# Splitting the attention projections' weights on GpSimd instead of VectorE

## The chip, the core and the metric

The program runs on one core of a Trainium2 chip. The metric is the device time of one execution, in microseconds (us). The engines are called PE (TensorE: matmuls, with PEld for its weight loads), DVE (VectorE), ACT (ScalarE), POOL (GpSimd) and SP (SyncE, which here issues most of the DMAs).

## What is computed

Two decoder layers for a prompt of 1024 tokens and for 8 sample tokens that share the weights. Each layer takes an RMS norm of x, projects it with one weight matrix, runs four heads of differential attention beside four heads of gated linear attention, projects the result back, and adds a SwiGLU block. The part that matters here is the projection of the four attention heads:

```python
n = rmsnorm(yp, norm1[l])          # (y * g): g is norm1, one value per input feature
z = n @ w_in_l                     # 1024 features in, D_IN columns out
dq, dk, dv, gq, gk, gv, gg, gr = jnp.split(z, cuts, axis=-1)
q = rope(rmsnorm(dq.reshape(B, T, DIFF_HEADS, 2, DIFF_DK), q_norm_l), pos)
k = rope(rmsnorm(dk.reshape(B, T, DIFF_HEADS, 2, DIFF_DK), k_norm_l), pos)
v = dv.reshape(B, T, DIFF_HEADS, DIFF_DV)
```

Each head needs 128 columns each of q, k and v. The kernel multiplies in a shortened float format (fp32r), so it splits both operands of each product in a high and a low part and adds three products: high by high, low by high, high by low.

## The kernel before

Each layer runs three stages one after the other. Stage D (`phase_d`, line 384) does the attention heads, stage G (`phase_g`) the gated linear attention, and stage F the output projection and the SwiGLU block, with the attention of the sample tokens over the paged cache laid beside it. In layer 0 stage D takes the time from the start to about 285 us, in layer 1 from about 1400 to 1666 us.

In stage D the heads come one after the other (line 586). For each head, `head(h)` (line 403) prepares the weights of the head, and returns three functions: `proj(i)` projects tile i of 128 tokens (i = 8 is the tile of the 8 sample tokens), `attend(i)` does the scores, the softmax and the product with v of tile i, and `finish` normalises the head's output. The loop issues `proj(0)`, `proj(1)`, the sample tile, and `proj(2)` to `proj(7)`; two attention tiles stay pending (`LAG`, line 45), so the attention of tile i follows `proj(i + 2)`, and the last tiles of a head fall beside the first projections of the next. `head(h + 1)` is called behind `proj(3)` of head h.

The weights of a head are prepared by `prep_cols` (line 212) in eight steps, k = 0 to 7, one for each 128 input features. A step loads `raw`, 128 rows by 384 columns (400 for head 3, which also carries the 16 columns of the gate's low rank part, loaded by a second DMA), from SP's queue. ACT writes `wh = raw * g` rounded to fp32r, where g is one value for each partition out of `g1c`. DVE writes `wl = raw * g - wh` with one scalar_tensor_tensor (the helper `stt`, line 137, whose instructions the profile shows at line 138). There are 4 buffers of `raw`, and 9 each of `wh` and `wl`. So one step of the next head can be prepared ahead, and the other seven wait until the last projection of the head before, `proj(7)`, has read its eight steps one after the other; and the `raw` of a step is loaded when the split four steps earlier has been done.

`proj(i)` is `gemm_tok` (line 236): for each step k three matmuls into one accumulator of PSUM (`psq`; there are 3 of these), xH by wh, xL by wh, and xH by wl. What follows each projection on ACT and DVE are the squares, the norm and the rotation of q and k, the copy of v, and DMAs of k and v to the outputs; then PE transposes q and k.

The tile framework orders each engine's instructions when the program is built: it plans by priority (the order of the program text) among the instructions that its plan has as ready, and on the chip each engine then works through its list in that order. The order on PE, ACT, DVE, POOL and SP is thus fixed before the run, and it can come out otherwise when an instruction moves to another engine.

The helper `tt` (line 134) is a tensor_tensor, on DVE unless another engine is given; the profile shows its instructions at line 135. `bc` (line 140) broadcasts an operand.

Of the kernel before, what the change touches and what calls it, by code (L numbers as in the profile page):

```python
# [16 lines left out]
ALU = mybir.AluOpType  # L17
# [4 lines left out]
P = 128  # L22
# [20 lines left out]
RANK = 16  # L43
# [9 lines left out]
C_Q, C_K, C_V = 0, 512, 1024  # L53
# [4 lines left out]
def f(ap):  # L58
    return ap.bitcast(F32)
# [3 lines left out]
def hybrid_kernel(  # L63
# [8 lines left out]
    PE, ACT, DVE, POOL, SP = nc.tensor, nc.scalar, nc.vector, nc.gpsimd, nc.sync  # L72
# [14 lines left out]
    def act(out, in_, func, **kw):  # L87
        return ACT.activation(out, in_, func, **kw)  # L88
# [45 lines left out]
    def tt(out, a, b, op, eng=None):  # L134
        return (eng or DVE).tensor_tensor(out, a, b, op=op)  # L135

    def stt(out, in0, scalar, in1, op0, op1, eng=None):
        (eng or DVE).scalar_tensor_tensor(out=out, in0=in0, scalar=scalar, in1=in1, op0=op0, op1=op1)  # L138

    def bc(ap, shape):  # L140
        return ap.to_broadcast(shape)
# [67 lines left out]
            cols = slice(NT, NT + 1)  # L209
            col_stats(slice(0, NB), cols, ps[0:NB, cols], 1.0)  # L210

    def prep_cols(wps, l, c0, ns, w, step, q=SP, gr=False, width=None):
        Hs, Ls = [], []
        n = ns * w + (RANK if gr else 0)
        width = width or n
        for k in range(KD):
            raw = wps[0].tile([P, width], F32, name="raw", tag="raw", bufs=4)
            if ns == 1:
                q.dma_start(raw, w_in[l, k * P:(k + 1) * P, c0:c0 + w])
            else:  # L220
                b0 = c0 - c0 % step
                q.dma_start(raw[:, :ns * w].rearrange("p (s c) -> p s c", s=ns),
                            w_in[l, k * P:(k + 1) * P, b0:b0 + ns * step]
                            .rearrange("p (s c) -> p s c", s=ns)[:, :, c0 % step:c0 % step + w])
            if gr:
                q.dma_start(raw[:, ns * w:n], w_in[l, k * P:(k + 1) * P, C_GR:C_GR + RANK])
            wh = wps[1].tile([P, width], F32R, name="wh", tag="wh", bufs=9)
            wl = wps[2].tile([P, width], F32R, name="wl", tag="wl", bufs=9)
            g = g1c[:, l, k:k + 1]
            act(wh[:, :n], raw[:, :n], AF.Copy, scale=g)  # L230
            stt(wl[:, :n], raw[:, :n], g, f(wh[:, :n]), ALU.mult, ALU.subtract)
            Hs.append(wh)
            Ls.append(wl)
        return Hs, Ls
# [149 lines left out]
    def phase_d(l, dctx, sn, pgp):  # L384
        pp, dpa, wr, wh_, wl_, dpb = [dctx.enter_context(tc.tile_pool(name=n, bufs=1, reuse_waits="tile"))
                                      for n in ("dpp", "dpA", "wDr", "wDh", "wDl", "dpB")]
        wp = (wr, wh_, wl_)
# [15 lines left out]
        def head(h):  # L403
            has_gr = h == GRH
            nc_ = 384 + (RANK if has_gr else 0)
            Hs, Ls = prep_cols(wp, l, C_Q + h * P, 3, P, C_K - C_Q, gr=has_gr, width=384 + RANK)
            kt = [None, None]
            vts = []
            qts = {}
# [148 lines left out]
        if l == 0:  # L558
            load_x(dp, psS, (0, NT))
        heads = [head(0)]  # L560
        if l == 0:
            load_x(dp, psS, range(1, NT))
# [23 lines left out]
        for h in range(H):  # L586
            proj, attend, finish = heads[h]
            for i in (0, 1, NT, 2, 3, 4, 5, 6, 7):
                proj(i)
                if l and h == 0 and i == 0:  # L590
                    rms_cols(1, psT, "T")
                if i == 3 and h + 1 < H:
                    heads.append(head(h + 1))
                if i == 4 and h == 0:
                    rms_rows(dp, psT, "T", "sqo")
                if i < NT:
                    pending.append(lambda a=attend, i=i: a(i))
                while len(pending) > LAG:
                    pending.pop(0)()
            pending.append(finish)  # L600
# [5 lines left out]
    def phase_g(l, gctx, ogs, smc, gsm, wa2):  # L606
# [15 lines left out]
        def proj_qk(p, c):  # L622
            if p not in qws:
                qws[p] = prep_cols(wp, l, C_GQ + p * P, 2, P, C_GK - C_GQ, q=w_queues[0])
            Hs, Ls = qws[p]
            dst, s = gqs[p][c], (DK ** -0.5, 1.0)[c]
            for t, (a, b) in enumerate(PIECES):
                ps = psg.tile([P, 512], F32, name="psqk", tag="g")
                gemm_feat(ps, c * P, Hs, Ls, t)
                stt(dst[:, a:b], ps[:, :b - a], s, rstd[:, a:b], ALU.mult, ALU.mult)  # L630
# [26 lines left out]
        def proj_v(p, half):  # L657
            if half == 0:
                vws[p] = prep_cols(wp, l, C_GV + p * 256, 1, 256, 256, q=w_queues[1])
                gvs[p] = []  # L660
            Hs, Ls = vws[p]
            out = gvs[p]
            for i in range(5 * half, min(5 * half + 5, NT + 1)):
                ps = psg.tile([P, 512], F32, name="psv", tag="g")
                gemm_tok(ps, 256, Hs, Ls, i)
                if i < NT:
                    v = gp.tile([P, 256], F32, name="gv", tag="gv", bufs=8)
                    act(v, ps[:, :256], AF.Copy, scale=rcol[:, i:i + 1])
                    out.append(v)
                else:  # L670
                    z = gb_.tile([NB, 256], F32, name="gvz", tag="gsq", bufs=2)
                    act(z, ps[32:32 + NB, :256], AF.Copy)
                    tt(z, ps[0:NB, :256], z, ALU.add)
                    act(z, z, AF.Copy, scale=rcol[0:NB, NT:NT + 1])
                    SP.dma_start(scr_gv[l][:, p * 256:(p + 1) * 256], z)
# [657 lines left out]
```

## Time and profile before

| | |
|---|---|
| median of 3 runs | 2796.83 us (2789.23 to 2798.13) |
| profiled execution, its own time | 2795.14 us |
| its span, first to last instruction | 2793.3 us |
| mean granted TensorE clock | 0.989 of full speed |
| PE, PEld busy | 97%, 86% of the span |
| DVE, ACT, POOL busy | 65%, 49%, 14% |

The busy share is a mean over stages that differ, so the stretches in question have to be read by themselves. The views used below are the page's table of engines, sums over stretches (windows), groups of instructions (lines, tiles), instructions in order of time (timeline), and the chain of waits that ended last. A timeline row merges neighbouring instructions of one kind ("x4"), and tells in brackets how long the engine had been idle and what ended that.

### The profile page before, as it was taken

To read this page: it belongs to the slowest core of one execution; us is meant where nothing else is said; L and a number is where in the kernel's file an instruction comes from. 1 tells how busy PE (TensorE), PEld (TensorE's weight loads), DVE (VectorE), ACT (ScalarE), POOL (GpSimd) and SP (SyncE) were. 2 spreads that over 40 slices of the span, in tenths; PEclk is the share of its full clock that TensorE was granted. 3 is DMA by queue.
4 is the path that set the end of the run, shared out by engine and by line. 5 is a ranking of instruction groups with operands and counts; after the bars stand their busy time and mean duration, and the time that the engine had idled before them with its cause. 6 is when DMAs were issued, how large, how long until landed. Compare 5 with 4: busy or idle time off the path is not lost.

```text
span 2793.3 us, 46822 instructions
## 1 busy us (share of the span) xinstructions
PE 2709.5 (97%) x16906; PEld 2403.9 (86%) x16906; DVE 1824.9 (65%) x3549; ACT 1358.8 (49%) x3343; POOL 403.0 (14%) x333
## 2 busy tenths in 40 slices
PE   8999999999999999999999999999999999999999
PEld 6888788777888799999988878877788888999999
DVE  6777676788777664444477775777777775544444
ACT  7888545533454442222278884455324454322222
POOL 1000100145343100000020001002453430000000
PEclk9999999999999999999999999999999999999999
DMA  5111111356666342333212111124566665333332
GB/s 133 56 56 41 57 32 54 109 176 201 185 200 195 104 128 84 93 94 94 75 42 70 47 38 49 32 59 137 174 202 177 191 192 151 91 92 91 91 91 84
DMA packets 461322, 298.13 MB, mean 107 GB/s; under 512 B 34698, under 2 KB 416906, under 8 KB 461090
## 3 DMA queue, kind: packets, MB, share of 16 engines
q1 hardware_dynamic: 452322, 290.90, 35.4%
q10 hardware_dynamic: 8704, 4.20, 0.6%
q8 instruction: 134, 2.20, 0.3%
q14 instruction: 98, 0.80, 0.1%
q0 software_dynamic: 64, 0.03, 0.0%
HBM read 271.53 MB, written 23.53 MB: 106 GB/s over the span
## 4 chain that ended last, share of the span: by engine, by line
PE 78%; DVE 10%; ACT 8%; issue 2%; DMA 2%; SPq 0%; POOL 0%; ACTq 0%; DVEq 0%; POOLq 0%
PE psd L82 56%; PE psq L82 4%; PE psqk L82 3%; PE psv L82 3%; PE psgg L82 2%; PE po L82 2%; ACT sc L88 2%; PE psA L82 1%; DVE wl L135 1%; PE psS L82 1%; ACT qn L88 1%; PE poG L82 1%; ACT qhh L88 1%; PE tpw L85 1%; DVE acc L135 1%
## 5 line engine op out<-in xcount | busy, mean ns | idle before, releaser
L88 ACT ACTIVATE wh<-raw 128x512 fp32r<-128x512 f32 (+1 forms) x608 | 353.6, 615 | 909.3 <-PE psd L82 737.3
L82 PE MATMUL psd<-xH,wh 128*128 128x260 f32 (+1 forms) x2112 | 681.9, 323 | 3.6 <-ACT xH L88 3.5
L82 PE MATMUL psd<-xL,wh 128*128 128x260 f32 (+1 forms) x2112 | 679.9, 322 | 4.2 <-DVE xL L138 4.2
L82 PE MATMUL psd<-xH,wl 128*128 128x260 f32 (+1 forms) x2112 | 682.2, 323 | 0.9 <-DVE wl L135 0.9
L135 DVE TENSOR_TENSOR wl<-raw,wh 128x512 fp32r<-128x512 f32 (+1 forms) x608 | 443.9, 746 | 72.8 <-issue 41.3
L82 PEld LDWEIGHTS psd<-xL,wh 128*128 128x128 f32 x2112 | 400.2, 189 | 38.4 <-DVE xL L138 6.5
L82 PEld LDWEIGHTS psd<-xH,wh 128*128 128x128 f32 x2112 | 399.8, 189 | 36.3 <-ACT xH L88 4.4
L82 PEld LDWEIGHTS psd<-xH,wl 128*128 128x128 f32 x2112 | 400.3, 190 | 34.2 <-DVE wl L135 1.8
L82 PE MATMUL psd<-hh,wl 128*128 128x260 f32 (+1 forms) x1056 | 340.6, 323 | 6.1 <-DVE wl L135 6.0
L82 PE MATMUL psd<-hh,wh 128*128 128x260 f32 (+1 forms) x1056 | 338.8, 321 | 0.9 <-DVE acc L135 0.9
L82 PE MATMUL psd<-hl,wh 128*128 128x260 f32 (+1 forms) x1056 | 338.3, 320 | 0.0
L135 POOL TENSOR_TENSOR page<-page,qbd 128x512 f32<-128x512 f32 x128 | 190.5, 1504 | 307.9 <-DMA page<-in_cache_k 162.7
L135 DVE TENSOR_TENSOR acc<-psd,acc 128x520 f32<-128x520 f32 (+1 forms) x144 | 125.6, 872 | 150.7 <-PE psd L82 150.7
L82 PEld LDWEIGHTS psd<-hh,wl 128*128 128x128 f32 x1056 | 199.1, 189 | 25.8 <-DVE wl L135 12.0
L82 PEld LDWEIGHTS psd<-hh,wh 128*128 128x128 f32 x1056 | 199.2, 189 | 14.6 <-issue 1.3
L82 PEld LDWEIGHTS psd<-hl,wh 128*128 128x128 f32 x1056 | 198.8, 188 | 13.6
L82 PE MATMUL psq<-wh,xH 128*128 128x384 f32 (+1 forms) x512 | 180.0, 352 | 7.3 <-DVE zs L135 4.3
L135 DVE TENSOR_TENSOR sa<-psd,rstd 128x520 f32<-128x520 f32 (+1 forms) x66 | 57.7, 874 | 197.0 <-PE psd L82 194.7
L82 PE MATMUL psq<-wh,xL 128*128 128x384 f32 (+1 forms) x512 | 179.4, 351 | 0.0
L82 PE MATMUL psq<-wl,xH 128*128 128x384 f32 (+1 forms) x512 | 178.6, 349 | 0.0
L135 DVE TENSOR_TENSOR tb<-psd,rstd 128x520 f32<-128x520 f32 (+1 forms) x66 | 57.7, 874 | 165.9 <-PE psd L82 165.9
L138 DVE SCALAR_TENSOR_TENSOR wl<-raw,g1c,wh 128x256 fp32r<-128x256 f32 (+2 forms) x160 | 80.9, 536 | 73.5 <-ACT wh L88 72.8
(330 smaller groups left out, 5421.2 us busy)
## 6 DMA issues: line engine op xcount, KB each, us to landing
raw<-in_w_gu SPq DMA_DIRECT2D x176, 512.0 KB
raw<-in_w_down SPq DMA_DIRECT2D x160, 256.0 KB
page<-in_cache_k SPq DMA_DIRECT2D x128, 256.0 KB
page<-in_cache_v SPq DMA_DIRECT2D x128, 256.0 KB
raw<-in_w_out SPq DMA_DIRECT2D x32, 512.0 KB
raw<-in_w_in SPq DMA_DIRECT2D x64, 192.0 KB
raw<-in_w_in SPq DMA_DIRECT2D x64, 128.0 KB
xt<-in_x_prompt SPq DMA_DIRECT2D x8, 512.0 KB
```

The lines of the kernel that those rows point to most:

```text
L82: PE.matmul(out, lhsT=lhsT, rhs=rhs, start=start, stop=stop, skip_group_check=True)
L85: PE.matmul(out, lhsT=in_, rhs=ident[:n, :n], is_transpose=True)
L88: return ACT.activation(out, in_, func, **kw)
L135: return (eng or DVE).tensor_tensor(out, a, b, op=op)
L138: (eng or DVE).scalar_tensor_tensor(out=out, in0=in0, scalar=scalar, in1=in1, op0=op0, op1=op1)
```

## The change

`prep_cols` gets an argument `pool`. Where it is set, `wl` is made on POOL by two instructions: a product in place, `raw = raw * g`, with g broadcast along the columns, and a subtraction, `wl = raw - wh`. The product writes over `raw`, which ACT reads for `wh`, so it comes behind ACT's instruction. `phase_d` sets the argument for heads 1 to 3; head 0, stage G and stage F stay as they were. That makes 3 heads x 8 steps x 2 layers = 48 splits that move.

```diff
-    def prep_cols(wps, l, c0, ns, w, step, q=SP, gr=False, width=None):
+    def prep_cols(wps, l, c0, ns, w, step, q=SP, gr=False, width=None, pool=False):
...
             act(wh[:, :n], raw[:, :n], AF.Copy, scale=g)
-            stt(wl[:, :n], raw[:, :n], g, f(wh[:, :n]), ALU.mult, ALU.subtract)
+            if pool:
+                tt(raw[:, :n], raw[:, :n], bc(g, [P, n]), ALU.mult, POOL)
+                tt(wl[:, :n], raw[:, :n], f(wh[:, :n]), ALU.subtract, POOL)
+            else:
+                stt(wl[:, :n], raw[:, :n], g, f(wh[:, :n]), ALU.mult, ALU.subtract)
...
-            Hs, Ls = prep_cols(wp, l, C_Q + h * P, 3, P, C_K - C_Q, gr=has_gr, width=384 + RANK)
+            Hs, Ls = prep_cols(wp, l, C_Q + h * P, 3, P, C_K - C_Q, gr=has_gr, width=384 + RANK, pool=h > 0)
```

## Rows read from the trace of the kernel before

**Rows 1.** The page: its span, and busy us (share of the span) xinstructions by engine.
```profile
span 2793.3 us, 46822 instructions
...
PE 2709.5 (97%) x16906; PEld 2403.9 (86%) x16906; DVE 1824.9 (65%) x3549; ACT 1358.8 (49%) x3343; POOL 403.0 (14%) x333
```
**Rows 2.** Windows, busy us by engine: heads 1 to 3 of both layers, summed.
```profile
sum 395.40, PE 383.70 PEld 330.56 DVE 304.51 ACT 343.22 POOL 0.00; mean PE 63.95 PEld 55.09 DVE 50.75 ACT 57.20 POOL 0.00
```
**Rows 3.** Windows: the six head changes, 20 us from the first split on, summed.
```profile
sum 120.00, PE 115.49 PEld 101.84 DVE 109.32 ACT 110.41 POOL 0.00; mean PE 19.25 PEld 16.97 DVE 18.22 ACT 18.40 POOL 0.00
```
**Rows 4.** Tile wl: instructions, ns min/median/max, first and last start in us, forms.
```profile
L138 DVE SCALAR_TENSOR_TENSOR wl<-raw,g1c,wh x160: 448/484/637, 11.1 to 1880.5; 128x256 fp32r<-128x256 f32 x96, 128x384 fp32r<-128x384 f32 x48, 128x400 fp32r<-128x400 f32 x16
```
**Rows 5.** Timeline of DVE, second head change: start us, us, instruction, count, [idle before].
```profile
143.61 2.21 DVE L138 SCALAR_TENSOR_TENSOR wl<-raw,g1c,wh 128x384 fp32r<-128x384 f32 x4 [1.06 <-ACT wh L88]
147.68 0.62 DVE L138 SCALAR_TENSOR_TENSOR wl<-raw,g1c,wh 128x384 fp32r<-128x384 f32 x1
...
149.70 0.62 DVE L138 SCALAR_TENSOR_TENSOR wl<-raw,g1c,wh 128x384 fp32r<-128x384 f32 x1 [0.29 <-ACT wh L88]
```
**Rows 6.** Timeline of PE: last matmul with wl of proj(0); changes 1, 2, 6.
```profile
87.94 0.34 PE L82 MATMUL psq<-wl,xH 128*128 128x384 f32 x1
...
153.64 0.34 PE L82 MATMUL psq<-wl,xH 128*128 128x384 f32 x1
...
1604.99 0.35 PE L82 MATMUL psq<-wl,xH 128*128 128x400 f32 x1
```
**Rows 7.** Groups of POOL: engine, instruction, shapes, count | busy us, mean ns | idle.
```profile
L135 POOL TENSOR_TENSOR vaccp<-vaccp,page 128x512 f32<-128x512 f32 x48 | 73.3, 1528 | 163.7 <-ACT page L88 160.8 <-issue 2.8
...
L135 POOL TENSOR_TENSOR vb<-vb,smc 128x512 f32<-128x512 f32 x8 | 9.2, 1156 | 2.0 <-DMA vb<-scr_gv 2.0
...
L135 POOL TENSOR_TENSOR cg<-cg,gqk 128x512 f32<-128x512 f32 x4 | 5.1, 1278 | 32.3 <-DMA cg<-c_cos 32.3
...
L135 POOL TENSOR_TENSOR cg<-cg,gqk 8x64 f32<-8x64 f32 x4 | 1.2, 310 | 0.0
```
**Rows 8.** Timeline of ACT: the first wh of head changes 2 and 6.
```profile
142.97 2.12 ACT L88 ACTIVATE wh<-raw,g1c 128x384 fp32r<-128x384 f32 x4
...
1594.44 1.14 ACT L88 ACTIVATE wh<-raw,g1c 128x400 fp32r<-128x400 f32 x2
```
**Rows 9.** Chain of waits in order of time, first head change: start us, us, what.
```profile
77.36 0.61 ACT wh L88
...
78.53 0.64 DVE wl L138 x2
79.16 3.63 DMA raw<-in_w_in
...
82.82 0.62 ACT wh L88
...
83.47 0.62 DVE wl L138
...
84.74 0.90 DVE sc L138
...
85.78 0.74 PE tpw L85 x5
```
**Rows 10.** Timeline of POOL and DVE in stage F: a split beside GpSimd, one without.
```profile
657.00 1.29 POOL L135 TENSOR_TENSOR page<-page,qbd 128x512 f32<-128x512 f32 x1 [5.99 <-DMA page<-in_cache_k]
...
657.06 1.77 DVE L135 TENSOR_TENSOR wl<-raw,wh 128x512 fp32r<-128x512 f32 x1
659.35 0.67 DVE L135 TENSOR_TENSOR wl<-raw,wh 128x512 fp32r<-128x512 f32 x1
```
**Rows 11.** Groups of DVE with two SBUF inputs, 143.6 to 158.6 us.
```profile
L138 DVE SCALAR_TENSOR_TENSOR sc<-sc,rr 128x640 f32<-128x640 f32 x1 | 0.9, 884 | 0.0
...
L135 DVE TENSOR_TENSOR qk<-qk,t 128x256 f32<-128x256 f32 x1 | 0.4, 422 | 0.0
L135 DVE TENSOR_TENSOR qk<-qk,rs 128x256 f32<-128x256 f32 x1 | 0.4, 422 | 0.0
```

## The prediction

> **What bounds the kernel now.** I read the page's engine table first, then the stretches that the change touches, then the chain of waits in one of them. In the table PE is busy 97% of the span and GpSimd 14% [rows 1]; the reader is to see that PE sets the pace and GpSimd looks free. The sums over stretches narrow this down. Over heads 1 to 3 of both layers, 395.4 us, PE is busy 383.7, ACT 343.2, DVE 304.5 and GpSimd not at all [rows 2]. So in these heads PE can gain at most 395.4 - 383.7 = 11.7 us. The splits don't lie evenly in a head: seven of the eight come in one burst at the head change. In the 20 us from the first of these on, summed over the six changes (120 us), PE is busy 115.5, ACT 110.4 and DVE 109.3, that is 96, 92 and 91% [rows 3]: DVE is near full just where the change relieves it, but PE and ACT are too.
>
> The chain of waits at the first change shows what is late there [rows 9]: a wh of ACT (77.36), splits of DVE (to 79.17), the reload of raw that the freed buffer allows (3.63 us), again wh (82.82), the split (83.47), then DVE's sc (84.74) and the transposes tpw on PE (85.78). The weights' preparation itself is on the chain, through the four buffers of raw.
>
> **What goes.** 48 of the splits at line 138 leave DVE; the row of the tile holds 64 of this width, and 16 of them belong to head 0 [rows 4]. Back to back four take 2.21 us, 0.55 each [rows 5], so DVE is given 48 x 0.55 = 26.4 us, 4.4 in each change. What that can bring is bounded by PE's idle time: 120 - 115.5 = 4.5 us in the changes, 11.7 us in all.
>
> **What comes: GpSimd's pair.** The trace has no such instruction of 384 columns. A product with a broadcast operand on 512 columns took 1.278 us, and on 64 columns 0.310 [rows 7], so (1278 - 310)/448 = 2.16 ns for a column, and for 384 columns 0.310 + 320 x 0.00216 = 1.00 us, for 400 columns 1.04. Taking the subtraction alike, a pair is 2.00 us (2.07 for head 3) against DVE's 0.55. Bounds: at the quickest 512-column row (1.156) times 0.75 for both, 1.73; at the slowest that I take (1.528, a sum of two full tiles) 2.3 [rows 7]. I take 2.00, since cg is the nearest row: it ran with DVE quiet and one operand broadcast.
>
> A page puts this lower: the Trainium skill, GPSIMD Engine Reference, section Elementwise — side-by-side cycle accounting, gives some 2.6 cycles per element at 1.2 GHz, by which an estimate for the pair is 2 x 384 x 2.6 / 1.2 = 1.66 us. With it the delay summed below would be 6.4 us instead of 20.1; the row with its 2.16 ns a column has the measured price, and I keep that.
>
> **First delay: PE's need of the last split.** The seven pairs of a burst follow each other on one engine, and PE takes the steps in order. At the second change ACT's first wh of the burst starts at 142.97 [rows 8] and is done when DVE starts, at 143.61 [rows 5]. Seven pairs end at 143.6 + 14.0 = 157.6; PE uses the last wl at 153.64 [rows 6], so it would be 4.0 us late. DVE's last split now starts at 149.70 and ends at 150.32 [rows 5], 3.3 us ahead of use. At the first change the second wh of the burst ends only at 77.36 + 0.61 = 77.97 [rows 9], and six pairs from there give 89.97 against 87.94 [rows 6]: 2.0 late. At the sixth, 1594.44 + 0.62 = 1595.06 [rows 8], seven pairs of 2.07 give 1609.6 against 1604.99 [rows 6]: 4.6 late. The three changes between, by the same working, give 3.4, 4.0 and 2.1. The sum is 20.1 us.
>
> **Second delay: the reload of raw.** The raw of step k+4 is loaded when the split of step k has read its buffer, and ACT's wh stands in ACT's list behind that. Step 3 decides, since step 7 waits for it. At the first change DVE is done with step 3 at 79.17 [rows 9]; GpSimd would be at 77.97 + 2 x 2.00 = 81.97, 2.8 later, and the load, wh and all behind wh on ACT (exponentials, copies of transposes) move with it. At the second change DVE is done with it at about 143.61 + 3 x 0.55 = 145.3 [rows 5], GpSimd at 149.6: 4.3 later. The other four come to 4.5, 4.1, 4.3 and 4.3. SP's queue stops at each of these loads, with the outputs of q, k and v behind; two buffers of qk, tiles 395.4/54 = 7.3 us apart [rows 2], cover a stop of that size, so I count nothing for it. If they did not, DVE's next qk would wait, at most the 4.3 us already counted.
>
> The two delays lie at one place and don't add: while ACT is late, PE asks later. Taking the larger in each change, 2.8 + 4.3 + 4.5 + 4.1 + 4.3 + 4.6 = 24.6 us, if every engine kept its present order.
>
> **Contention between GpSimd and DVE.** In stage F a split of DVE that starts 0.06 us behind a GpSimd instruction takes 1.77 us, one without 0.67 [rows 10]: it is held for about the 1.29 us of the other. In a burst DVE has three to five instructions with two operands in SBUF (three rows here, 1.7 us [rows 11]; 25 over the six). If each is held half of a 1.00 us instruction, DVE loses 12.5 of the 26.4 us, and GpSimd waits for DVE's in turn for some 3 us in all. The Trainium skill, SBUF — State Buffer, section Who interferes with whom, has the rule behind this row, and it speaks against the change: a DVE instruction with two SBUF inputs and a GpSimd instruction that reads SBUF exclude each other for the whole instruction. The row agrees. By the row alone every DVE instruction of a burst could be held, and DVE's loss would be above its gain; by the rule only those with two SBUF inputs are.
>
> **The sum.** With the present order the delays are 24.6 + 3 = 27.6 us; this is the upper end. The lower end is -11.7, PE's whole idle time in these heads. For the value: DVE's relief takes at most the 4.5 us of PE's idle time in the changes from it, leaving 23.1. But the orders are planned anew, and the attention tiles 4 to 7 of the head before give PE, ACT and DVE work that needs no split. I take half as covered by that: 23.1 / 2 = 11.6 us. I don't go lower, because each head change has PE busy 96% already, and what PE loses there it can't regain behind it. Against the profiled execution's own 2795.1 this is 2806.7; the median of the runs is 1.7 above that execution, which gives 2808.
>
> **The rivals.**
> - Covered: the planner draws the attention tiles forward until the splits are there. For it: the last four attention tiles are pending at each change, and the delay is spread over six places. Against it: their pace is set by ACT and DVE, at 91 to 92% there [rows 3], so PE's work isn't ready sooner. Time: 2797, within 5.
> - Faster: DVE is what holds PE at the head change (PE stood idle until sc of DVE released tpw, [rows 9]), the pending tiles run faster without the splits, and GpSimd is in time. It decides where a pair is short enough: at the second change (153.64 - 143.61)/7 = 1.43 us, at the first (87.94 - 77.97)/6 = 1.66. Against it: no row of GpSimd with two inputs gives a pair so short [rows 7], unless the order moves. Worth 4.5 to 11.7 us; about 10: 2787.
> - In full: the orders stay, nothing covers, GpSimd and DVE hold each other up. 2796.8 + 27.6 = 2824.
> - That the splits don't get to GpSimd in time at all, because its queue is held by something else, I rule out: it runs nothing in these heads [rows 2].
>
> **How the numbers follow.** A measurement of this kernel tells about 0.3%, 8.4 us, from no change: under 2788.4 is faster, above 2805.2 slower. My forecast (partly covered, 2801 to 2818) has 0.45, covered 0.27, in full 0.15, faster 0.13. Of the forecast's 0.45 some 0.07 lies below 2805.2. Slower: 0.38 + 0.15 = 0.53; the same: 0.27 + 0.07 = 0.34; faster: 0.13. The range goes from 2788 to 2828, which leaves out most of the faster case and the tail of the full one.
>
> **What would show it.** In the trace after: GpSimd some 96 us busier (48 x 2.0), in six bursts of about 14 us or more; DVE with 48 splits fewer and some qk or sc instructions about twice as long; PE waiting at the head change for a wl of GpSimd, or ACT for raw, 2 to 4 us each, where now these waits are 1 us or less. The prediction is wrong if PE's idle time in the changes stays at 4.5 us in all (covered) or shrinks (faster), or if the pair takes less than 1.5 us.

## The result and the profile after

The changed kernel takes 2818.63 us (median of 5 runs, 2809.03 to 2823.59) against 2793.22 for the kernel before (5 runs, 2784.78 to 2798.13): the ratio is 1.0089, with a 95% interval of 1.0072 to 1.0106, or 25 us slower (20 to 30). The profiled execution took 2809.03, the quickest of the five; its span is 14 us longer than that of before, so the traces show the places, and the sizes in us are taken from the ratios. The five runs follow TensorE's granted clock: from 2809.03 us at a mean of 0.993 of full speed to 2823.59 at 0.987.

The page after: span, busy us by engine, and the chain that ended last by engine; the first two answer to [rows 1].

```profile
span 2807.3 us, 46933 instructions
...
PE 2704.6 (96%) x16906; PEld 2395.9 (85%) x16906; DVE 1805.2 (64%) x3501; ACT 1360.7 (48%) x3343; POOL 492.2 (18%) x429
...
PE 75%; DVE 11%; ACT 7%; issue 4%; DMA 2%; POOL 1%; SPq 0%; ACTq 0%; DVEq 0%; POOLq 0%
```

DVE lost its 48 splits (3549 - 3501) and GpSimd has 96 instructions and 89 us more. The 26 us of work that left DVE show as only 20 us less of busy time. The two sums over stretches, first heads 1 to 3 of both layers as in [rows 2], then the six head changes, 20 us each from the first split on, as in [rows 3]:

```profile
sum 417.00, PE 388.33 PEld 330.82 DVE 293.75 ACT 344.65 POOL 77.99; mean PE 64.72 PEld 55.14 DVE 48.96 ACT 57.44 POOL 13.00
```
```profile
sum 120.00, PE 97.83 PEld 84.00 DVE 78.56 ACT 96.94 POOL 86.50; mean PE 16.31 PEld 14.00 DVE 13.09 ACT 16.16 POOL 14.42
```

The heads take 417.0 us in place of 395.4, 21.6 longer; that the span is only 14 longer is due to later stages, which the change leaves alone and where this execution was quicker, within the spread of the runs. PE's idle time in the changes is 22.2 us where it was 4.5, ACT's 23.1 where it was 9.6, and DVE's 41.4 where it was 10.7. No engine is near full any more: they wait for each other. GpSimd's own instructions, as groups (busy us, mean ns | idle before):

```profile
L135 POOL TENSOR_TENSOR wl<-raw,wh 128x384 fp32r<-128x384 f32 x32 | 33.4, 1050 | 1.9
...
L135 POOL TENSOR_TENSOR raw<-raw,g1c 128x384 f32<-128x384 f32 x32 | 27.6, 867 | 235.8 <-ACT wh L88 138.9 <-DMA raw<-in_w_in 59.4 <-PE tpqk L85 37.6
...
L135 POOL TENSOR_TENSOR wl<-raw,wh 128x400 fp32r<-128x400 f32 x16 | 17.3, 1088 | 0.9
...
L135 POOL TENSOR_TENSOR raw<-raw,g1c 128x400 f32<-128x400 f32 x16 | 14.5, 910 | 106.6 <-ACT wh L88 57.4 <-PE psq L82 49.2
```

A pair takes 0.867 + 1.050 = 1.92 us. One head change from close by, the second, as in [rows 5]. The timeline of GpSimd, of DVE and of PE:

```profile
150.68 1.61 POOL L135 TENSOR_TENSOR raw<-raw,g1c 128x384 f32<-128x384 f32 x2
152.26 1.97 POOL L135 TENSOR_TENSOR wl<-raw,wh 128x384 fp32r<-128x384 f32 x2
...
155.09 1.46 POOL L135 TENSOR_TENSOR wl<-raw,wh 128x384 fp32r<-128x384 f32 x1
...
159.47 1.00 POOL L135 TENSOR_TENSOR wl<-raw,wh 128x384 fp32r<-128x384 f32 x1
...
154.74 0.95 DVE L138 SCALAR_TENSOR_TENSOR sc<-sc,rr 128x640 f32<-128x640 f32 x1 [2.19 <-ACT sc L88]
...
159.68 1.08 DVE L135 TENSOR_TENSOR qk<-qk,rs 128x256 f32<-128x256 f32 x1 [0.97 <-ACT rs L88]
...
155.84 0.73 PE L85 MATMUL tpw<-ident,sc 128*128 128x128 f32 x5 [1.99 <-DVE sc L138]
...
160.53 0.44 PE L82 MATMUL psq<-wl,xH 128*128 128x384 f32 x1 [1.26 <-POOL wl L135]
```

The reader is to see both kinds of contact. DVE's qk<-qk,rs, 0.42 us long in [rows 11], takes 1.08: it begins 0.21 us behind a GpSimd subtraction of 1.00. And a GpSimd subtraction that meets DVE's sc at 155.09 takes 1.46 in place of about 1.0. PE stands idle twice, for sc of DVE and for a split of GpSimd. The chain of waits in order of time names what lies behind the first of these, and answers to [rows 9]:

```profile
149.70 1.04 POOL wl L135
...
150.75 2.52 DMA raw<-in_w_in
...
153.38 0.62 ACT wh L88
153.99 0.73 ACT sc L88
...
154.74 0.96 DVE sc L138
...
155.84 0.64 PE tpw L85 x4
```

The split frees raw late, the load comes late, ACT's wh stands in ACT's list waiting for it, the exponential of the attention stands behind wh, and PE's transposes behind that.

### The profile page after: what moved, and what is told of

The parts are those of the page before. It is cut to its first block, busy times and chain, and to the rows that moved or that the text cites. A ratio compares the mean times of both kernels' runs of the same rounds, so it can differ in the third digit from the quotient of the medians.

```text
span 2807.3 us, 46933 instructions
## 1 busy us (share of the span) xinstructions
PE 2704.6 (96%) x16906; PEld 2395.9 (85%) x16906; DVE 1805.2 (64%) x3501; ACT 1360.7 (48%) x3343; POOL 492.2 (18%) x429
## 4 chain that ended last, share of the span: by engine, by line
PE 75%; DVE 11%; ACT 7%; issue 4%; DMA 2%; POOL 1%; SPq 0%; ACTq 0%; DVEq 0%; POOLq 0%
PE psd L82 55%; PE psqk L82 3%; PE psv L82 3%; PE psq L82 3%; PE psgg L82 2%; PE po L82 2%; ACT sc L88 2%; DVE wl L135 1%; PE psA L82 1%; ACT qn L88 1%; PE poG L82 1%; PE tpw L85 1%; DVE sc L508 1%; ACT qhh L88 1%; DVE acc L135 1%
## 5 line engine op out<-in xcount | busy, mean ns | idle before, releaser
L82 PEld LDWEIGHTS psd<-hh,wl 128*128 128x128 f32 x1056 | 198.6, 188 | 26.7 <-DVE wl L135 12.9
L82 PEld LDWEIGHTS psq<-wh,xH 128*128 128x128 f32 x512 | 96.8, 189 | 10.5 <-issue 4.9
```

The costliest lines, as they stand in the source:

```text
L82: PE.matmul(out, lhsT=lhsT, rhs=rhs, start=start, stop=stop, skip_group_check=True)
```

## The experiments

Each ran beside the kernel before. "Held" is my sum over one trace, from 60 to 300 and from 1440 to 1690 us: for each DVE instruction with two operands in SBUF, its time above the median of the same instruction in the kernel before, where that is over 0.05 us. It is 0 in the kernel before and 11.8 us (25 instructions) in the changed one. What GpSimd holds ahead of these two stretches, at the first step that is split early, isn't counted: 0.6 us in the changed kernel, 0.2 to 2.5 us in the others, and with 13 buffers 4.6. In us, a ratio is taken times 2793.

**Lateness alone.**

```diff
+            if pool:
+                for _ in range(5):
+                    POOL.memset(f(wl[:, :n]), 0.0)
             stt(wl[:, :n], raw[:, :n], g, f(wh[:, :n]), ALU.mult, ALU.subtract)
```


> The splits stay on VectorE as in the kernel before, but ahead of each split of heads 1 to 3 GpSimd fills that wl five times (about 2.1 us), and the split waits for it. GpSimd reads nothing and VectorE is relieved of nothing: lateness alone. Lateness theory (the seven splits of a head change come 2 to 5 us behind PE's need): 15 to 27 us slower than before, as the change. Contention theory (GpSimd and VectorE hold each other up at SBUF): within 5 us of before, since only instructions that read are held.

Ratio 0.9989 (0.9979 to 0.9999), 3 us quicker; held 0. The splits were as late as they are in the changed kernel: at the second change the last one ends 13.9 us behind the end of the first wh, and 13.6 in the changed kernel. The sum over the six changes, and then the fills as a group:

```profile
sum 120.00, PE 116.31 PEld 102.24 DVE 101.26 ACT 106.72 POOL 85.13; mean PE 19.38 PEld 17.04 DVE 16.88 ACT 17.79 POOL 14.19
```
```profile
L233 POOL MEMSET wl<- 128x384 f32 (+1 forms) x240 | 90.1, 424 | 320.9 <-PE psq L82 276.4 <-PE psd L82 42.6
```

PE is as busy as before (116.3 and 115.5), with GpSimd busy 85 us in these 120. The order of PE's matmuls in the trace is another than in the kernel before (a comparison of the two lists of 16906, by names and shapes, has some 700 lines of difference), and with that order the lateness of the splits is covered. The reload of raw is covered too. These are ACT's waits for raw in the two layers (us in total, times, longest), first in the changed kernel, then with the fills ahead of unchanged splits:

```profile
ACT wh L88 <- DMA raw<-in_w_in: 6.2, 4, 1.9
ACT wh L88 <- DMA raw<-in_w_in: 3.0, 3, 1.3
```
```profile
ACT wh L88 <- DMA raw<-in_w_in: 1.1, 2, 0.7
ACT wh L88 <- DMA raw<-in_w_in: 0.8, 2, 0.5
```

So splits that end late cost nothing by themselves, under an order of their own. That lateness costs nothing under the changed kernel's order isn't shown by this run.

**GpSimd's reads alone.**

```diff
             stt(wl[:, :n], raw[:, :n], g, f(wh[:, :n]), ALU.mult, ALU.subtract)
+            if pool:
+                scr = wps[0].tile([P, width], F32, name="scr", tag="scr", bufs=1)
+                tt(scr[:, :n], f(wh[:, :n]), bc(g, [P, n]), ALU.mult, POOL)
+                tt(scr[:, :n], scr[:, :n], f(wh[:, :n]), ALU.subtract, POOL)
```


> The splits stay on VectorE, and beside each of heads 1 to 3 GpSimd runs the change's two instructions into a spare tile that nobody reads (product of wh with g, then minus wh). GpSimd's load and contention without lateness. Lateness theory: within 5 us of before. Contention theory: 15 to 27 us slower, or more than the change, since VectorE also keeps its splits.

Ratio 1.0093 (1.0077 to 1.0109), 26 us slower, the whole loss of the change; held 30.1 us, of which 20.0 on the splits. Nothing waits for these instructions' results, and the order of the instructions on PE, ACT and DVE in the trace is that of the kernel before, one by one, by names and shapes. The second head change in this trace (timeline of DVE and then of GpSimd), and the sum over the six changes:

```profile
147.67 4.11 DVE L138 SCALAR_TENSOR_TENSOR wl<-raw,g1c,wh 128x384 fp32r<-128x384 f32 x4 [1.06 <-ACT wh L88]
...
147.78 1.20 POOL L135 TENSOR_TENSOR scr<-wh,g1c 128x384 f32<-128x384 f32 x1 [53.48 <-ACT wh L88]
149.05 1.21 POOL L135 TENSOR_TENSOR scr<-scr,wh 128x384 f32<-128x384 f32 x1
```
```profile
sum 120.00, PE 95.56 PEld 82.20 DVE 115.44 ACT 92.19 POOL 99.77; mean PE 15.93 PEld 13.70 DVE 19.24 ACT 15.36 POOL 16.63
```

Four splits take 4.11 us in place of 2.21 [rows 5]: DVE and GpSimd take turns. PE loses 20 us of work in the changes without one wait of its own for GpSimd. DVE's other instructions in these heads, with at most one operand in SBUF, keep their length: none is more than 0.05 us above its median.

**The same reads, shorter and with one operand.** The first cuts each spare instruction in two halves of the columns, the second runs two copies of wh.

```diff
-                tt(scr[:, :n], f(wh[:, :n]), bc(g, [P, n]), ALU.mult, POOL)
-                tt(scr[:, :n], scr[:, :n], f(wh[:, :n]), ALU.subtract, POOL)
+                for c in (slice(0, n // 2), slice(n // 2, n)):
+                    tt(scr[:, c], f(wh[:, c]), bc(g, [P, n // 2]), ALU.mult, POOL)
+                    tt(scr[:, c], scr[:, c], f(wh[:, c]), ALU.subtract, POOL)
```


> The run with spare GpSimd work beside unchanged splits, with each of its instructions cut in two halves of the columns. If VectorE waits for the end of the GpSimd instruction it meets: the time held falls from 30 us to 15 to 22, and the loss from 26 us to 12 to 20. If it is the share of time in which GpSimd reads that counts: 24 us or more stay, since the halves take longer in sum.

```diff
+                POOL.tensor_copy(scr[:, :n], f(wh[:, :n]))
+                POOL.tensor_copy(scr[:, :n], f(wh[:, :n]))
```


> The same with two copies of wh into the spare tile in place of the product and the subtraction: GpSimd reads one operand per instruction. If any GpSimd instruction that reads SBUF holds VectorE's instructions with two inputs for its length: a loss in proportion to the copies' length, 10 to 26 us. If only GpSimd instructions with two operands do: within 4 us of before.

Halves: 1.0035 (1.0023 to 1.0047), 10 us, held 18.8, though GpSimd's time in these heads rises from 100 to 127 us. Copies of some 0.65 us each: 1.0025 (1.0014 to 1.0036), 7 us, held 10.9. So it isn't the share of time in which GpSimd works that counts but the length of the instruction that DVE meets, and one operand is enough. The order of the instructions is that of before in these two as well. The halves cost less than I had expected, and the copies' 7 us lie between my two expectations, within 4 and 10 to 26; that they hold DVE at all is read from the trace.

**Relief and lateness without reads, and relief alone.** Five fills in place of the pair, then one.

```diff
-                tt(raw[:, :n], raw[:, :n], bc(g, [P, n]), ALU.mult, POOL)
-                tt(wl[:, :n], raw[:, :n], f(wh[:, :n]), ALU.subtract, POOL)
+                for _ in range(5):
+                    POOL.memset(f(wl[:, :n]), 0.0)
```


> As the changed kernel, but in place of GpSimd's pair it fills wl five times with zeros (about 2.1 us, which leaves the low part of the weights of heads 1 to 3 out): VectorE is relieved and the wl come as late as in the changed kernel, but GpSimd reads nothing. Contention theory: within 5 us of before or a little faster, the 25 us gone. Lateness theory, which the run with delayed splits already speaks against: 10 us or more slower.

```diff
+                POOL.memset(f(wl[:, :n]), 0.0)
```


> The same with one fill of some 0.43 us, which leaves the low part out as well: VectorE's relief of 26 us alone, without lateness and without reads of GpSimd. If VectorE holds PE up at the head changes: 5 to 12 us faster than before. If PE bounds these heads by itself: within 4 us.

1.0010 (1.0001 to 1.0018) and 1.0012 (1.0001 to 1.0022): 3 us slower each, held 0. The same lines of DVE's groups, layer 1 from 1468 to 1690 us, in the changed kernel and with five fills:

```profile
L135 DVE TENSOR_TENSOR qk<-qk,rs 128x256 f32<-128x256 f32 (+1 forms) x29 | 14.7, 505 | 1.9 <-ACT rs L88 0.9 <-ACT v L88 0.5
L135 DVE TENSOR_TENSOR qk<-qk,t 128x256 f32<-128x256 f32 (+1 forms) x29 | 13.0, 447 | 0.3
```
```profile
L135 DVE TENSOR_TENSOR qk<-qk,rs 128x256 f32<-128x256 f32 (+1 forms) x28 | 11.8, 420 | 4.8 <-ACT rs L88 4.0
L135 DVE TENSOR_TENSOR qk<-qk,t 128x256 f32<-128x256 f32 (+1 forms) x27 | 11.3, 418 | 0.3
```

With fills, GpSimd is busy at least as long as in the change (240 fills of 0.42 us), and DVE's instructions have their old length of 0.42 us. And the relief of 26 us on DVE brings the kernel nothing, even with neither lateness nor contention. In the trace with one fill stage D, from the copies to xs to the last ol, is some 3 us shorter than before (301.4 + 281.9 us in the two layers against 303.0 + 283.5), so it may be worth that much there. One thing differs from the change beside the reads: a fill doesn't read raw, so raw comes free when ACT has read it, and its reload isn't late (ACT waits 2.0 us for it with five fills, 9.2 in the changed kernel). Five fills test the late splits, not the late reload.

**Lateness taken away, reads kept.** 13 buffers of wh and wl in the attention heads, in the changed kernel and, as a control, in the kernel before.

```diff
-            wh = wps[1].tile([P, width], F32R, name="wh", tag="wh", bufs=9)
-            wl = wps[2].tile([P, width], F32R, name="wl", tag="wl", bufs=9)
+            wh = wps[1].tile([P, width], F32R, name="wh", tag="wh", bufs=13 if width == 384 + RANK else 9)
+            wl = wps[2].tile([P, width], F32R, name="wl", tag="wl", bufs=13 if width == 384 + RANK else 9)
```


> The changed kernel with 13 buffers of wh and of wl in place of 9 in the attention heads: five steps of the next head can be split ahead and three are left for the head change, 6 us of GpSimd in place of 14. Lateness theory: the 25 us are gone, within 6 us of before, perhaps faster. Contention theory: the same GpSimd instructions beside VectorE, so 10 us or more stay. Plan theory (the new order of instructions costs by itself): 10 us or more may stay as well.

> The kernel before (splits on VectorE) with 13 buffers of wh and wl in the attention heads: what the buffers do by themselves. Contention theory: within 5 us of before or faster, so that the 13 us of the changed kernel with 13 buffers are GpSimd's. If instead the new plan that comes with 13 buffers costs the 13 us: as slow as that one.

The changed kernel with 13 buffers: 1.0046 (1.0031 to 1.0061), 13 us; held 12.9, and 4.6 more ahead of the two stretches, since four more steps are split early. Its last wl is 4 us or more ahead of PE's use at each change, and the tile's answer has no one who waited for wl:

```profile
L135 POOL TENSOR_TENSOR wl<-raw,wh x48: 996/1043/1607, 45.8 to 1608.8; 128x384 fp32r<-128x384 f32 x32, 128x400 fp32r<-128x400 f32 x16
its engine sat idle before it (us, times) until:
who waited for it (us, times):
```

The control: 1.0001 (0.9991 to 1.0010). So the buffers and the plan that comes with them cost nothing on DVE, and the 13 us are GpSimd's reads. The 12 us between this and the changed kernel went when the lateness was taken away; as the order of the instructions changed with it, and no run has the changed kernel's order with splits in time, what the order costs by itself stays open.

**The reload of raw.** 8 buffers of raw in place of 4.

```diff
-            raw = wps[0].tile([P, width], F32, name="raw", tag="raw", bufs=4)
+            raw = wps[0].tile([P, width], F32, name="raw", tag="raw", bufs=8 if width == 384 + RANK else 4)
```


> The changed kernel with 8 buffers of raw in place of 4 in the attention heads: the load of a step no longer waits for GpSimd's split four steps earlier. If the reload of raw (through wh on ACT) is the larger of the two delays: 5 to 13 us slower than before in place of 25. If PE's wait for the last wl is: 18 us or more stay, since GpSimd's seven pairs take as long as they did.

1.0097 (1.0081 to 1.0114), 27 us; held 12.0. The reload is gone, and the wait turns up at the next place. PE's waits, longest in total first (us in total, times, longest), from 60 to 300 us and from 1440 to 1690:

```profile
PE psq L82 <- POOL wl L135: 8.6, 6, 2.5
```
```profile
PE psq L82 <- POOL wl L135: 9.1, 6, 2.5
```

PE waits 17.7 us in all for GpSimd's splits, 12 times over the six changes; in the changed kernel that is 4.6 us, and in the kernel before PE waited for no split there. So the late split has taken the place of the late reload. But the 27 us are not all its price, and there is no control with 8 buffers and the splits on DVE. First, the buffers also move the preparation of head 0 in layer 1, from about 1030 us to 1420: its eight splits now run on DVE beside GpSimd's products for cg and sg, PE waits 4.2 us for them, and the time from the copies to xs to the first rotation of q and k is 12.6 us, 6.4 in the kernel before. Second, the granted clock falls to half, 1.2 GHz, seven times in stage D after its first 30 us, for 30.6 us in all (10.2 in the kernel before). The first of these (stretch, its length, busy us of PE, PEld, DVE, ACT and POOL, granted clock, DMA):

```profile
88.70:92.10 3.40, 3.17 (x9) 2.77 (x10) 1.15 (x4) 1.21 (x9) 1.97 (x3) 0.50 0.51 135
```

Ahead of it PE had stood idle 2.11 and 1.05 us for splits of GpSimd. All five runs with 8 buffers have a mean clock of 0.985 to 0.988, the kernel before has 0.988 to 0.993. An estimate from the changed kernel's own runs, 14.6 us for 0.006 of clock: some 10 of the 27 us.

**Part of it, and the product first.**

```diff
-            if pool:
+            if pool and k % 2 == 0:
                 tt(raw[:, :n], raw[:, :n], bc(g, [P, n]), ALU.mult, POOL)
```


> The change for the even steps of heads 1 to 3 only: 24 splits on GpSimd, 24 on VectorE, bursts of three or four pairs, 6 to 8 us. Contention theory: collisions in proportion, 8 to 14 us slower than before, more if VectorE's odd splits are held too. Lateness theory: within 4 us of before, since the burst fits into the slack that the splits have now.

```diff
-            act(wh[:, :n], raw[:, :n], AF.Copy, scale=g)
             if pool:
                 tt(raw[:, :n], raw[:, :n], bc(g, [P, n]), ALU.mult, POOL)
+                act(wh[:, :n], raw[:, :n], AF.Copy)
                 tt(wl[:, :n], raw[:, :n], f(wh[:, :n]), ALU.subtract, POOL)
             else:
+                act(wh[:, :n], raw[:, :n], AF.Copy, scale=g)
```


> The changed kernel with GpSimd's product ahead of ACT's wh (which then only rounds raw): the product of the four steps whose raw is already loaded leaves the burst at the head change. The same GpSimd instructions, so VectorE is held as in the changed kernel (some 12 us); less lateness. If about half of the change's 25 us is lateness beyond what the order of PE and ACT allows for: 11 to 18 us slower than before. If all of it is contention: 20 to 28. If all of it were lateness: 0 to 8.

Half of the splits: 1.0022 (1.0013 to 1.0031), 6 us, held 6.1; less than contention in proportion, more than nothing. Product first: 1.0056 (1.0041 to 1.0070), 16 us, held 10.5; within the range for a loss that is part contention and part lateness.

All runs, ordered by the time that DVE was held:

| kernel | held, us | slower, us |
|---|---|---|
| lateness alone; five fills; one fill; 13 buffers before | 0 | -3; 3; 3; 0 |
| half of the splits | 6.1 | 6 |
| product first | 10.5 | 16 |
| spare copies | 10.9 | 7 |
| the change | 11.8 | 25 |
| 8 buffers of raw | 12.0 | 27 |
| 13 buffers | 12.9 (17.5 with the early steps) | 13 |
| spare halves | 18.8 | 10 |
| spare pairs | 30.1 | 26 |

No kernel in which GpSimd doesn't read lost more than 3 us, and none in which it does was as quick as before. Where nobody waits for GpSimd's results in time (13 buffers, spare work, half), the loss is 0.5 to 1.0 of the time held; the change loses 13 us more than it is held. The 8 buffers of raw lose 15 more, of which some 10 go with the clock and up to 6, in part the same, with head 0 of layer 1.

## Why the prediction held, and where it didn't

The direction and the range held: 2808 was forecast, 2788 to 2828 as the range, 2818.6 measured. But the gain of a few us to PE that I set against the delays didn't come, and the measured 25 us lie next to the rival "in full", 27.6. My own sum gave 11 us, less than half of what was measured, so it is in part the luck of a wide range that the time lies in it. By its steps:

- **The pair.** Forecast 2.00 us, measured 1.92, and by the medians, mostly undisturbed, 0.83 + 1.03 = 1.86. The page that I had weighed against the row (the Trainium skill, GPSIMD Engine Reference, section Elementwise — side-by-side cycle accounting) gives 0.83 us for one such instruction as an estimate; the product agrees with it and the subtraction is a fifth longer. The delay a third as long that I had worked out from it didn't follow: the pair of 1.86 to 1.92 us lies nearer to my 2.00 than to that estimate's 1.66.
- **The burst.** 14.0 us forecast from the end of the first wh to the end of the last split at the second change; 13.6 measured.
- **First delay.** PE does wait for the last wl there, 1.26 us in one wait; over both layers these waits come to 4.6 us, where I had 20.1 for an order that stays. The order didn't stay.
- **Second delay.** The chain after goes exactly through it: split, reload, wh, sc, tpw, with 1.99 us of idle PE. ACT waits 9.2 us in all for raw (6.2 and 3.0 us in the two layers), 2.8 before. I had said that the two delays lie at one place and don't add; the run with 8 buffers of raw agrees, since without the second the first takes its place (17.7 us of PE's waits in place of 4.6); its time can't be set against the change's, because of its clock and of head 0.
- **Contention.** DVE's held time was forecast at 12.5 us and is 11.8. What I mis-sized is its worth: I counted 3 us of it in the sum, GpSimd's share, and set DVE's share off against DVE's relief. The runs in which nobody waits for GpSimd show that a held DVE instruction is a loss of 0.5 to 1 us for each us, and the single fill that DVE's relief, which I had put at up to 4.5 us, brings the kernel nothing. The rule of the Trainium skill (SBUF — State Buffer, section Who interferes with whom) spoke against the change and was right in each part that the runs touch: only instructions with two SBUF inputs were held (30.1 us with spare pairs, no other instruction by more than 0.05 us), fills that only write held none, and the length of the instruction met is what is paid (18.8 us with halves).
- **Cover.** Half was forecast for planned order against delay. The runs show it otherwise: with splits as late but GpSimd not reading, all of the lateness is covered (0.9989, ACT's waits for raw 1.9 us), and with the pairs a part isn't (9.2 us of ACT's waits for raw, 4.6 of PE's for splits).

So the theory that I held at the start, lateness, fell as the sole cause; contention explains some 13 of the 25 us (13 buffers). The other 12 went with the lateness, but that it is lateness alone, and not the order of the changed kernel, is argued from the waits of PE and ACT and not shown. Why the order covers the fills and not the pairs is not shown either. Two reasons are open: the plan may have the pair shorter than 1.92 us, or the held instructions on both engines shift what the plan had fitted together. No run took the one from the other. A small part may be the clock: the change's runs have a mean of 0.990, those of the kernel before 0.991, by the estimate above 2 to 4 us.

## What to carry to other kernels

An idle GpSimd isn't free: look first at how many VectorE instructions near it read two operands from SBUF, and count the time they are held as lost where all engines are tight, without setting it off against work taken from VectorE. Relief of an engine that is 91% busy, beside one at 96%, brought this kernel nothing; a kernel that leaves the moved work out, as the single fill did, prices the relief in one run. And where a moved producer comes late, ask whether the consumers' order is planned for it: a burst of 14 us that only wrote cost nothing under the order that came with it, and one that also read lost some 12 us beyond its contention under another. And read the granted clock beside the time: waits of PE can cost more than their own length.

## What the runs showed of the hardware

- A GpSimd copy, with one operand, holds VectorE's instructions with two SBUF operands as well: 96 copies of 0.65 us held them 10.9 us. Fills (480 of 0.42 us in two runs) held none.
- The same GpSimd work in instructions half as long held VectorE 18.8 us in place of 30.1, although it took 27 us more of GpSimd's time. Where such work must run beside VectorE, shorter instructions are the cheaper form.
- The granted clock fell to half, 1.2 GHz, for 3.4 or 6.8 us at a time; with 8 buffers of raw five of the seven falls lie at head changes, where PE waited for splits of GpSimd, and two at the start of layer 1.
- GpSimd is held in turn: its product, 0.83 us undisturbed, took up to 1.44 us, and its subtraction up to 1.51 us.
